# Context tokens of a diffusion layer: one pair of k tiles turned at once, the other seven in a lane beside the products

## The chip, the cores and the metric

The kernel runs on one core of a Trainium2 chip. A time is the device time of one execution in microseconds (us). The engines of the core are TensorE (PE; its weight loads are shown as PEld), VectorE (DVE), ScalarE (ACT), GpSimd (POOL) and SyncE (SP), which issues nearly all transfers. They run side by side and wait for each other by semaphores.

## The reference

One layer of a diffusion model for 256 latent tokens `x` and 256 context tokens `ctx`, width D = 2048, in float32. The part that the change touches is the first one: all 512 tokens are normalised by their root mean square, scaled and shifted by terms that are computed from a condition vector, and multiplied by one wide weight matrix.

```python
def rms_norm(x, g):
    y = xf * lax.rsqrt(jnp.mean(xf * xf, axis=-1, keepdims=True) + NORM_EPS)
    return y * g
def modulate(h, shift, scale):
    return h * (1 + scale) + shift
def ada_terms(cond, w_ada, b_ada):
    return jnp.split(jax.nn.silu(cond) @ w_ada + b_ada, 6, axis=-1)
# c conditions the latent tokens, c_ctx the context tokens
# z = modulate(rms_norm(tokens, norm1_g), shift, scale);  proj = z @ w_in
# columns of w_in: keys and values (latent and context tokens) | queries | gates (latent only)
```

Behind it come two kinds of attention of the latent tokens over all 512 tokens, a gated merge, a second normalisation and a gated MLP with a convolution of width 3. Their code is the same in both kernels.

## The kernel before

**Tiling.** A k tile is 128 of the 2048 rows of `w_in`; there are 16. Tokens come in with the tokens on the partitions, so each 128 x 128 piece has to be turned by PE (a matmul with the identity `ident`, L227) before it can be an operand whose contraction runs over D. The turned and normalised tokens `xn` lie in the slots X0 to X3, four k tiles each, latent and context side by side. A pair of k tiles of the context takes four transposes into one PSUM bank (two k tiles by two halves of the tokens) and then one scaling on DVE by `rb`, the reciprocal root mean square spread over the partitions.

**Products.** Each float32 operand is split in two parts, `hi` (a rounded copy, made by ACT) and `lo` (the rest, a DVE subtraction), and each product is the sum of three matmuls, hi x hi, hi x lo, lo x hi (`mm` at L218). The weights pass through a ring of four raw buffers (`raw`) and three buffers each of `hi` and `lo`. In the trace `sZL` is the modulated operand of the latent tokens, `sZC` that of the context tokens; `make_z` makes both parts of each: for each k tile ACT makes hi, DVE multiplies in place, DVE subtracts.

**Chunks and blocks.** The k tiles are taken in five chunks of 2, 3, 3, 4 and 4 tiles. In each chunk the blocks of columns follow each other: `a` and `b` (keys and values, both kinds of token), `c` and `d` (queries) and the gate blocks `0` to `3`. Chunk 0 has the order `cd012ab3`, the next two `abcd0123`, chunk 3 `abcd`, chunk 4 begins with `b` and `d`. Block results are added up in SBUF by DVE (evacuations such as `sK<-bank,sK`).

**Modulation values.** For each chunk a GEMV (`gemv_chunk`) takes the columns of `w_ada` for the chunk's k tiles through the same ring of raw buffers and multiplies them with the condition vectors `cs` (L409 in the rows, four steps for a chunk of three or four tiles), after which ACT copies the sums to `scratch`, PE turns them (`bank<-ident,scratch`) and three DVE operations make `md`, the shift and scale of that chunk. `make_z` of a chunk can't begin before its `md`.

**What sets the order.** PE's instructions stand in the order in which the program emits them. A small planner (`Pace`) interleaves side jobs, called lanes, with the products: it keeps a model of the work that DVE and ACT still have, lets it shrink by the modelled time of each product, and takes a step of a lane where the modelled rest of DVE and of ACT is at most the lane's limit and where a distance that the lane asked for by its last `yield` has passed on PE. Lanes of smaller `prio` go first. `finish` runs a lane to its end at once. Lanes of the first chunks are `lane_ctx` (the context's preparation), `lane_mods` (GEMV steps, with a distance of 4, 10, 14 and 14 us between the steps of chunks 1 to 4) and `lane_z` (the operands of the next chunk). The order on DVE and ACT follows from a scheduler that goes by the emitted order and the dependencies.

In chunk 0 the context's tokens are loaded ahead of gate block 0 and `lane_ctx` is added; the lane is finished ahead of block `a`, the first that needs it. In chunk 0, `lane_mods` and `lane_z` are added at the same place. A chunk ends with

```python
        while ci + 1 not in mods:
            next(gm)
        finish(nxt)
```

so that GEMV steps which found no place between the blocks, and what is left of the next operands, are emitted there in one go.

Of the kernel before, what the change touches and what calls it, by code (L numbers as in the profile page):

```python
# [9 lines left out]
F32 = mybir.dt.float32  # L10
# [6 lines left out]
P = 128  # L17
D = 2048
KT = D // P
T = 256  # L20
# [9 lines left out]
CHUNKS = (2, 3, 3, 4, 4)  # L30
# [3 lines left out]

ORDER0, ORDERM, CTX_AT = "cd012ab3", "abcd0123", 2

CTX_LIM, NXT_LIM, GM_LIM, LIM_EVAC, LIM_ATT, LIM_LAT = 0.1, 0.8, 2.0, 2.0, 3.0, 1.3
REST_LIM, REST_LIM_B, REST_LIM_Q, REST_LIM_A, REST_LIM_W, REST_LIM_U = 0.65, 0.6, 1.7, 0.5, 1.4, 0.5
REST_CI, REST_AFTER, REST_DMA = 1, 6.0, 6.0
GAPS = (0.0, 4.0, 10.0, 14.0, 14.0)  # L40
# [10 lines left out]
class Pace:  # L51
# [50 lines left out]
    def run(self, gen):  # L102
        for _ in gen:
            self.tick()

    def finish(self, *gens):

        gens = list(gens)
        self.lanes = [x for x in self.lanes if not any(x[0] is g for g in gens)]
        while gens:  # L110
            gens = [g for g in gens if next(g, None) is not None]
# [39 lines left out]
def _build(tc, nc, es, a):  # L151
    pace = Pace()
    PE, POOL = nc.tensor, nc.gpsimd
    ACT, DVE = Engine(nc.scalar, pace, "act"), Engine(nc.vector, pace, "dve")
    run, finish = pace.run, pace.finish
# [5 lines left out]
    tmp = es.enter_context(tc.tile_pool(name="tmp", bufs=3))  # L161
    psum = es.enter_context(tc.tile_pool(name="psum", bufs=8, space=bass.MemoryType.PSUM))

    def bank():
        return psum.tile([P, 512], F32, tag="bank", name="bank")

    def slot(tag, shape, dt=F32):
        return big.tile(shape, dt, tag=tag, name=f"s{tag}")

    def small(n, tag="st", bufs=8):  # L170
        return tmp.tile([P, n], F32, tag=tag, name=tag, bufs=bufs)

    def scratch(shape, dt=F32):
        return tmp.tile(shape, dt, tag="P", name="scratch", bufs=4)
# [40 lines left out]
    def mm(out, lhsT, rhs, start, stop):  # L215
        n = free(rhs)
        pace.tensor(n * 0.417e-3 if rhs.dtype == F32R else max(n, 256) * 1.67e-3)
        PE.matmul(out, lhsT, rhs, start=start, stop=stop, skip_group_check=True)  # L218
# [6 lines left out]
    def transpose(out, src, n=P):  # L225
        pace.tensor(0.11)
        PE.transpose(out, src, ident[:n, :n])  # L227
# [16 lines left out]
    def rstd(out, sums, n, cnt, extra=None):  # L244
        m = small(8)
        DVE.tensor_scalar(out=m[:, :n], in0=sums, scalar1=1.0 / cnt, scalar2=EPS, op0=ALU.mult, op1=ALU.add)
        POOL.tensor_tensor(out=out, in0=m[:, :n], in1=mhalf[:, :n], op=ALU.pow)
        if extra is not None:
            DVE.tensor_scalar(out=out, in0=out, scalar1=extra, scalar2=None, op0=ALU.mult)


    xin = [slot(g, [P, D]) for g in ("ZC0", "K2", "G2", "G3")]

    def load_tokens(cnd):
        src = a["ctx"][0] if cnd else a["x"][0]
# [10 lines left out]
    def silu_c():  # L266
        ex = tmp.tile([P, 2, 16], F32, tag="cex", bufs=1, name="cex")
        ACT.activation(ex, craw, AF.Exp, scale=-1.0)
        DVE.tensor_scalar(out=ex, in0=ex, scalar1=1.0, scalar2=None, op0=ALU.add)
        DVE.reciprocal(ex, ex)  # L270
        DVE.tensor_mul(cs.rearrange("p j c -> p c j")[:, 0:2, :], craw, ex)
# [55 lines left out]
    xn = [slot(f"X{i}", [P, 4, NTOK]) for i in range(4)]  # L327

    def norm_tokens(cnd, fills=None):
        rb = scratch([P, T])  # L330
        rr = []

        def spread(t, ss):
            r = small(1)
            rstd(r, ss, 1, D)
            rt = tmp.tile([P, P], F32, tag="rr", name="rr", bufs=2)
            DVE.tensor_copy(rt, r.broadcast_to([P, P]))
            rr.append(rt)

        for t in range(2):  # L340
            ss = small(1)
            if cnd == 0:
                junk = slot(f"G{t}", [P, D])
                ACT.activation(junk, xin[t], AF.Square, accum_out=ss)
            else:
                s4 = small(4)
                for i in range(4):
                    ACT.activation(scratch([P, 512]), xin[2 + t][:, i * 512:(i + 1) * 512], AF.Square,
                                   accum_out=s4[:, i:i + 1])
                    yield 0.0  # L350
                DVE.reduce_sum(ss, s4, axis=AX.X)
            spread(t, ss)

        def turn(k2):
            ps = bank()
            for k in range(2):
                for t in range(2):
                    transpose(ps[:, (2 * k + t) * P:(2 * k + t + 1) * P],
                              xin[2 * cnd + t][:, (k2 + k) * P:(k2 + k + 1) * P])
            return k2, ps  # L360

        def scale(k2, ps):
            DVE.tensor_mul(xn[k2 // 4][:, k2 % 4:k2 % 4 + 2, cnd * T:(cnd + 1) * T],
                           ps.rearrange("p (k t) -> p k t", t=T), rb[:, None, :].broadcast_to([P, 2, T]))

        ahead = 2 if cnd == 0 else 1
        pend = [turn(k2) for k2 in range(0, 2 * ahead, 2)]
        yield 4.0
        if cnd == 0:
            silu_c()  # L370
        rbp = bank()
        for t in range(2):
            mm(rbp[:, t * P:(t + 1) * P], rr[t], ident, t == 0, True)
        ACT.copy(rb, rbp[:, 0:T])
        yield 1.0
        if cnd == 0:

            fills.extend((turn, scale, k2) for k2 in range(2 * ahead, KT, 2))
        for k2 in () if cnd == 0 else range(2 * ahead, KT, 2):
            scale(*pend.pop(0))  # L380
            pend.append(turn(k2))
            yield 0.5
        for p in pend:
            scale(*p)
            yield 0.0

    w_ada = a["w_ada"][0].rearrange("(p j) c -> p j c", j=16)
    starts = [sum(CHUNKS[:i]) for i in range(len(CHUNKS))]
# [44 lines left out]
    def make_z(ci, cnd):  # L433
        kt0, nk = starts[ci], CHUNKS[ci]
        md = mods[ci]
        zt = slot(("ZL", "ZC")[cnd] + str(ci % 2), [P, 2, nk, T], F32R)
        zs[ci][cnd] = zt
        c = slice(cnd * T, (cnd + 1) * T)
        for k in range(nk):
            kt = kt0 + k  # L440
            x = xn[kt // 4][:, kt % 4, c]
            s1, s2 = md[:, 1, k, cnd:cnd + 1], md[:, 0, k, cnd:cnd + 1]
            ACT.activation(zt[:, 0, k, :], x, AF.Identity, bias=s2, scale=s1)
            DVE.tensor_scalar(out=x, in0=x, scalar1=s1, scalar2=s2, op0=ALU.mult, op1=ALU.add)
            DVE.tensor_sub(zt[:, 1, k, :], x, zt[:, 0, k, :].bitcast(F32))
            if late:
                l, src, h = late.pop()
                DVE.tensor_sub(l, src, h.bitcast(F32))
            yield 0.0
# [87 lines left out]
    def group_T(ps, w, mov, first, last):  # L537
        wh, wl = w
        mh, ml = mov
        for n in range(wh.shape[1] // P):  # L540
            mm3(ps[n // 2][:, (n % 2) * T:(n % 2 + 1) * T], wh[:, n * P:(n + 1) * P], wl[:, n * P:(n + 1) * P],
                mh, ml, first and n % 2 == 0, last)
# [97 lines left out]
    def block_g(cis, g):  # L640
        if cis[0] == 0:
            gates[g] = slot(f"G{g}", [P, 8, T])
        ps = [bank() for _ in range(4)]
        ks = [(ci, k) for ci in cis for k in range(CHUNKS[ci])]
        for i, (ci, k) in enumerate(ks):
            group_T(ps, take(), zk(zs[ci][0], k), i == 0, i == len(ks) - 1)
            yield
        evac(f"g{g}", cis[0] == 0, [(gview(g, n), ps[n]) for n in range(4)])
# [77 lines left out]
    def lane_z(ci):  # L726
        while ci not in mods:
            yield 0.3
        for cnd in range(2):
            yield from make_z(ci, cnd)  # L730

    with tc.manual_schedule(engines={ENG.DVE, ENG.Activation}):
        fills, turned = [], []
# [24 lines left out]
        for scale, p in turned:  # L758
            scale(*p)

    def lane_ctx():
        yield from norm_tokens(1)
        yield from make_z(0, 1)

    gm = lane_mods()
    for ci in range(nch - 1):
        nxt = lane_z(ci + 1)
        lc = None
        if ci > 0:
            pace.add(nxt, limit=NXT_LIM)  # L770
        if ci == REST_CI:
            pace.add(rest, after=REST_AFTER, limit=REST_LIM, dma=REST_DMA, prio=9)
        if ci == 2:
            pace.add(lane_tables(), after=5.0, limit=1.0, prio=8)
        for i, b in enumerate(order(ci)):
            if ci == 0 and i == CTX_AT:
                load_tokens(1)
                lc = pace.add(lane_ctx(), after=CTX_AFTER, limit=CTX_LIM, prio=0)
                pace.add(gm, limit=GM_LIM, prio=2)
                pace.add(nxt, limit=NXT_LIM)  # L780
            if lc is not None and b in "ab":
                finish(lc)
                lc = None
            run(block_g([ci], int(b)) if b in "0123" else {"a": block_a, "b": block_b, "c": block_c, "d": block_d}[b](ci))
        while ci + 1 not in mods:
            next(gm)
        finish(nxt)
    last = nch - 1
    zo, zl_ = f"ZL{nch % 2}", f"ZL{last % 2}"
# [735 lines left out]
```

## Time and profile before

| | |
|---|---|
| time, median of 3 runs | 1538.22 us (1536.16 to 1539.11) |
| the profiled execution | 1534.41 us, of it the span of the trace 1532.6 us |
| PE busy | 1501.6 us, 98% of the span |
| PEld, DVE, ACT, POOL busy | 86%, 72%, 50%, 1% |
| DMA, main queue | 348.96 MB, 65.4% of 16 engines' span |

How to read it: busy is the time in which an engine had an instruction, whatever the others did. PE and PEld overlap. Times in a timeline count from the start of the span; ends of matmuls are modelled, so two neighbours on PE can overlap on paper, and the distance from one start to the next is the better measure of what one costs.

### The profile page before, as it was taken

To read this page: it belongs to the slowest core of one execution; us is meant where nothing else is said; L and a number is where in the kernel's file an instruction comes from. 1 tells how busy PE (TensorE), PEld (TensorE's weight loads), DVE (VectorE), ACT (ScalarE), POOL (GpSimd) and SP (SyncE) were. 2 spreads that over 40 slices of the span, in tenths; PEclk is the share of its full clock that TensorE was granted. 3 is DMA by queue.
4 is the path that set the end of the run, shared out by engine and by line. 5 is a ranking of instruction groups with operands and counts; after the bars stand their busy time and mean duration, and the time that the engine had idled before them with its cause. 6 is when DMAs were issued, how large, how long until landed. Compare 5 with 4: busy or idle time off the path is not lost.

```text
span 1532.6 us, 23197 instructions
## 1 busy us (share of the span) xinstructions
PE 1501.6 (98%) x9361; PEld 1316.5 (86%) x9361; DVE 1099.8 (72%) x1554; ACT 764.3 (50%) x1144; POOL 15.2 (1%) x23
## 2 busy tenths in 40 slices
PE   7999999999999999999989999999999999999997
PEld 5788888899999999998889888888888888888885
DVE  4457786798778887788878989667656666555556
ACT  4534242455775446643456545555545555444444
POOL 0000000010000000000000000000000000000000
PEclk9999999999999999999999999999999999999999
DMA  9779788655347784498957878655565565555552
GB/s 361 248 271 337 280 311 300 244 183 193 111 158 241 270 291 154 148 319 295 347 209 247 302 266 291 212 193 183 174 198 188 175 209 189 194 194 192 192 196 79
DMA packets 123708, 350.44 MB, mean 229 GB/s; under 512 B 6750, under 2 KB 20296, under 8 KB 117072
## 3 DMA queue, kind: packets, MB, share of 16 engines
q1 hardware_dynamic: 123600, 348.96, 65.4%
q8 instruction: 73, 1.20, 0.3%
q14 instruction: 35, 0.29, 0.1%
HBM read 346.84 MB, written 2.10 MB: 228 GB/s over the span
## 4 chain that ended last, share of the span: by engine, by line
PE 91%; DMA 4%; DVE 3%; ACT 1%; issue 1%; SPq 0%; ACTq 0%; POOLq 0%; POOL 0%; DVEq 0%
PE bank L218 88%; DMA raw<-in_w_ada 2%; PE bank L227 2%; PE bank L409 2%; DVE sK L140 1%; DVE acc L140 1%; ACT scratch L140 0%; DVE lo L140 0%; DMA sK<-in_x 0%; DMA raw<-in_w_in 0%; DMA raw<-in_w_out 0%; DVE sX L140 0%; DVE scratch L140 0%; ACT hi L140 0%; SPq L403 0%
## 5 line engine op out<-in xcount | busy, mean ns | idle before, releaser
L140 ACT CAST hi<-raw 128x1024 fp32r<-128x1024 f32 (+2 forms) x462 | 470.9, 1022 | 580.0 <-PE bank L218 511.9
L140 DVE TENSOR_TENSOR lo<-raw,hi 128x1024 fp32r<-128x1024 f32 (+2 forms) x463 | 548.0, 1187 | 294.0 <-ACT hi L140 292.8
L218 PE MATMUL bank<-sZL,hi 128*128 128x256 f32 (+2 forms) x2528 | 536.8, 313 | 1.3 <-ACT sZL L140 0.9
L218 PEld LDWEIGHTS bank<-sZL,hi 128*128 128x128 f32 (+1 forms) x2528 | 408.3, 191 | 28.8 <-issue 8.4
L218 PE MATMUL bank<-sZL,lo 128*128 128x256 f32 (+1 forms) x1648 | 386.9, 283 | 0.5 <-DVE lo L140 0.4
L218 PEld LDWEIGHTS bank<-sZL,lo 128*128 128x128 f32 (+1 forms) x1648 | 290.7, 190 | 14.6 <-DVE lo L140 0.9
L218 PE MATMUL bank<-hi,sZC 128*128 128x512 f32 (+1 forms) x816 | 261.2, 383 | 0.0
L218 PE MATMUL bank<-sX,hi 128*128 128x512 f32 (+1 forms) x896 | 235.1, 364 | 0.0
L218 PEld LDWEIGHTS bank<-hi,sZC 128*128 128x128 f32 x816 | 152.5, 188 | 30.0
L218 PEld LDWEIGHTS bank<-sX,hi 128*128 128x128 f32 x896 | 154.0, 190 | 15.6 <-issue 1.0
L140 DVE SCALAR_TENSOR_TENSOR acc<-raw,cs,acc 128x1024 f32<-128x1024 f32 x120 | 153.5, 1279 | 15.6 <-DMA raw<-in_w_ada 14.9
L218 PE MATMUL bank<-lo,sZC 128*128 128x512 f32 (+1 forms) x344 | 131.3, 382 | 0.0
L218 PEld LDWEIGHTS bank<-sX,lo 128*128 128x128 f32 x704 | 110.5, 189 | 13.6
L218 PE MATMUL bank<-sX,lo 128*128 128x256 f32 x704 | 119.9, 281 | 0.0
L218 PEld LDWEIGHTS bank<-lo,sZC 128*128 128x128 f32 x344 | 64.7, 188 | 12.4 <-DVE lo L140 0.2
L140 DVE TENSOR_TENSOR sK<-bank,sK 128x512 f32<-128x512 f32 (+1 forms) x92 | 60.0, 683 | 8.8 <-PE bank L218 6.4
L218 PE MATMUL bank<-hi,sZL 128*128 128x512 f32 x192 | 63.3, 392 | 0.0
L218 PE MATMUL bank<-sZC,hi 128*128 128x256 f32 x256 | 50.2, 283 | 1.4 <-DVE sZC L140 1.4
L218 PE MATMUL bank<-hi,sX 128*128 128x512 f32 x128 | 50.6, 396 | 0.0
L218 PE MATMUL bank<-lo,sX 128*128 128x512 f32 x128 | 50.1, 392 | 0.1
L140 DVE TENSOR_TENSOR sG<-bank,sG 128x512 f32<-128x512 f32 x64 | 41.6, 681 | 3.9 <-PE bank L218 3.9
L218 PEld LDWEIGHTS bank<-hi,sZL 128*128 128x128 f32 x192 | 36.1, 188 | 9.4 <-ACT hi L140 1.2
(203 smaller groups left out, 1397.6 us busy)
## 6 DMA issues: line engine op xcount, KB each, us to landing
raw<-in_w_up SPq DMA_DIRECT2D x88, 1024.0 KB, 5.0
raw<-in_w_ada SPq DMA_DIRECT2D x80, 1024.0 KB, 7.1
raw<-in_w_down SPq DMA_DIRECT2D x44, 1024.0 KB, 5.4
raw<-in_w_in SPq DMA_DIRECT2D x37, 1024.0 KB, 5.4
raw<-in_w_out SPq DMA_DIRECT2D x16, 1024.0 KB, 7.1
raw<-in_w_ada SPq DMA_DIRECT2D x16, 768.0 KB, 5.7
raw<-in_w_br_b SPq DMA_DIRECT2D x8, 1024.0 KB, 5.9
raw<-in_w_br_a SPq DMA_DIRECT2D x8, 1024.0 KB, 5.6
```

Source lines behind the costliest of these rows:

```text
L140: return f(*args, **kw)
L218: PE.matmul(out, lhsT, rhs, start=start, stop=stop, skip_group_check=True)
L227: PE.transpose(out, src, ident[:n, :n])
L409: PE.matmul(ps[32 * g:32 * g + 32, :cols], cs[:, j0 + jj, :], w[:, jj, :], start=j0 + j == 0, stop=j0 + j == 14, skip_group_check=True)
```

## The change

The limit of the context's lane goes from 0.1 to 1.0. The raw context's first half lies in the slot Y0 and no longer in G2 (which gate block 2 evacuates into), and `rb` gets a tile of its own, as it now lives longer. `norm_tokens(1)` turns and scales one pair of k tiles only, those of chunk 0; the other seven pairs go to a list. A new lane takes the pairs of that list one by one (turn, a distance of 1.0, scale, a distance of 0.5). It is added where `lane_ctx` has been finished, and run to its end behind the last block of chunk 0. `lane_z` waits, before it makes the context's operands of a chunk, until the k tiles of that chunk are turned.

```diff
-CTX_LIM, NXT_LIM, GM_LIM, ... = 0.1, 0.8, 2.0, ...
+CTX_LIM, NXT_LIM, GM_LIM, ... = 1.0, 0.8, 2.0, ...
-    xin = [slot(g, [P, D]) for g in ("ZC0", "K2", "G2", "G3")]
+    xin = [slot(g, [P, D]) for g in ("ZC0", "K2", "Y0", "G3")]
     def norm_tokens(cnd, fills=None):
-        rb = scratch([P, T])
+        rb = tmp.tile([P, T], F32, tag="rb", bufs=1, name="rb")
...
-        ahead = 2 if cnd == 0 else 1
-        pend = [turn(k2) for k2 in range(0, 2 * ahead, 2)]
+        pend = [turn(k2) for k2 in ((0, 2) if cnd == 0 else (0,))]
...
-        if cnd == 0:
-            fills.extend((turn, scale, k2) for k2 in range(2 * ahead, KT, 2))
-        for k2 in () if cnd == 0 else range(2 * ahead, KT, 2):
-            scale(*pend.pop(0))
-            pend.append(turn(k2))
-            yield 0.5
+        fills.extend((turn, scale, k2) for k2 in range(2 * len(pend), KT, 2))
         for p in pend:
             scale(*p)
             yield 0.0
     def lane_z(ci):
...
         for cnd in range(2):
+            while cnd and ctx_turned[0] < starts[ci] + CHUNKS[ci]:
+                yield 0.3
             yield from make_z(ci, cnd)
+    ctx_turned, more_ctx = [2], []
     def lane_ctx():
-        yield from norm_tokens(1)
+        yield from norm_tokens(1, more_ctx)
         yield from make_z(0, 1)
+    def lane_ctx_more():
+        while more_ctx:
+            turn, scale, k2 = more_ctx.pop(0)
+            p = turn(k2)
+            yield 1.0
+            scale(*p)
+            ctx_turned[0] = k2 + 2
+            yield 0.5
...
             if lc is not None and b in "ab":
                 finish(lc)
                 lc = None
+                more = pace.add(lane_ctx_more(), limit=1.0, prio=1)
...
         while ci + 1 not in mods:
             next(gm)
+        if ci == 0:
+            finish(more)
         finish(nxt)
```

The first place at which the order moves is the end of gate block 2 of chunk 0, where the preparation of the context is finished. Before, PE turns seven pairs of k tiles there (28 transposes) between the `rr` products that spread the reciprocal root mean square and the first product with `sZC`; now it does no transposes of its own there beside the four of the first pair, and four more stand behind block `a`, four behind block `b` and twenty at the end of the chunk. The GEMV's second step for chunk 1 (the eight products with `raw,cs`, 32x384) moves from behind gate block 1 to behind gate block 2.

The second place is the end of chunk 0 on PE: gate block 3, the last block, and what stands behind it. `sZL_248` is the latent operand of chunk 0, `sZL_848` or `sZL_890` and `sZC_925` are those of chunk 1, and `sY`, `sG` the two halves of the raw context. Before:

```order
L218 MATMUL bank<-sZL_248,hi 128x256 x2
L218 MATMUL bank<-sZL_248,lo 128x256
L218 MATMUL bank<-sZL_848,hi 128x256 x2
L218 MATMUL bank<-sZL_848,lo 128x256
L218 MATMUL bank<-sZC_925,hi 128x256 x2
```

Now:

```order
L218 MATMUL bank<-sZL_248,hi 128x256 x2
L218 MATMUL bank<-sZL_248,lo 128x256
L227 MATMUL bank<-ident,sY_90 128x128
L227 MATMUL bank<-ident,sG_91 128x128
L227 MATMUL bank<-ident,sY_90 128x128
L227 MATMUL bank<-ident,sG_91 128x128
L227 MATMUL bank<-ident,scratch 128x128 x3
L403 MATMUL bank<-raw,cs 32x384 x8
L227 MATMUL bank<-ident,sY_90 128x128
L227 MATMUL bank<-ident,sG_91 128x128
```

Behind these rows the last two go on in turn until sixteen transposes of the context have followed the GEMV's products, and then come `sZL_890` and `sZC_925`. The transposes of the modulation values (`ident,scratch`) and a GEMV step of the next chunk, which before stood ahead of gate block 3, now stand behind it.

The same place on DVE, where `lo` is the low part of a weight, `sX` the normalised tokens and `rb` the spread reciprocal. Before:

```order
L140 TENSOR_TENSOR md_831<-bank_827,vec_98 128x2x6
L140 TENSOR_TENSOR md_831<-bank_827,md_831 128x2x6
L140 SCALAR_TENSOR_TENSOR md_831<-md_831,vec_98 128x6
L140 TENSOR_TENSOR lo_863<-raw_860,hi_862 128x576
L140 TENSOR_SCALAR sX0_104<-sX0_104,md_831 128x256 x2
L140 TENSOR_TENSOR sZL1_848<-sX0_104,sZL1_848 128x256 x2
L140 TENSOR_SCALAR sX1_105<-sX1_105,md_831 128x256
L140 TENSOR_SCALAR sX0_104<-sX0_104,md_831 128x256
L140 TENSOR_TENSOR sZL1_848<-sX1_105,sZL1_848 128x256
L140 TENSOR_TENSOR sZC1_925<-sX0_104,sZC1_925 128x256
```

Now:

```order
L140 TENSOR_TENSOR sX1_105<-bank_862,rb_424 128x2x256
L140 TENSOR_TENSOR md_873<-bank_869,vec_98 128x2x6
L140 TENSOR_TENSOR lo_943<-raw_940,hi_942 128x576
L140 TENSOR_TENSOR md_873<-bank_869,md_873 128x2x6
L140 SCALAR_TENSOR_TENSOR md_873<-md_873,vec_98 128x6
L140 TENSOR_TENSOR sX2_106<-bank_898,rb_424 128x2x256
L140 TENSOR_SCALAR sX0_104<-sX0_104,md_873 128x256 x2
L140 TENSOR_TENSOR sZL1_890<-sX0_104,sZL1_890 128x256 x2
L140 TENSOR_TENSOR sX2_106<-bank_904,rb_424 128x2x256
L140 TENSOR_TENSOR sX3_107<-bank_910,rb_424 128x2x256
L140 TENSOR_TENSOR sX3_107<-bank_916,rb_424 128x2x256
L140 TENSOR_SCALAR sX1_105<-sX1_105,md_873 128x256
```

Five scalings of the context (`bank,rb`) now stand among the operations that make the operands of chunk 1, and `sZC1_925` comes three rows behind the last row shown, after `sX0` and `sZL1`.

The third place is the end of chunk 3 on PE, block `d`, whose latent operand is `sZL_2191` before and `sZL_2324` now. Before:

```order
L218 MATMUL bank<-lo,sZL_2191 128x512
L218 MATMUL bank<-hi,sZL_2191 128x512
L227 MATMUL bank<-ident,scratch 128x128 x4
L218 MATMUL bank<-hi,sZL_2191 128x512
L218 MATMUL bank<-lo,sZL_2191 128x512
```

Now, with `sZL_3011` the first operand of chunk 4:

```order
L218 MATMUL bank<-lo,sZL_2324 128x512
L218 MATMUL bank<-hi,sZL_2324 128x512
L227 MATMUL bank<-ident,scratch 128x128 x4
L218 MATMUL bank<-hi,sZL_3011 128x512
L218 MATMUL bank<-lo,sZL_3011 128x512
```

Before, 24 products of block `d` follow the transposes of the modulation values; now none does.

DVE at the end of chunk 3, with `sK` the evacuations of blocks and `acc` the accumulation of another GEMV. Before:

```order
L140 TENSOR_TENSOR lo_2944<-raw_2922,hi_2943 128x1024
L140 TENSOR_TENSOR md_2966<-bank_2961,vec_98 128x16
L140 TENSOR_TENSOR md_2966<-bank_2961,md_2966 128x16
L140 SCALAR_TENSOR_TENSOR md_2966<-md_2966,vec_98 128x8
L140 TENSOR_TENSOR lo_2980<-raw_2977,hi_2979 128x1024
L140 TENSOR_SCALAR sX3_107<-sX3_107,md_2966 128x256 x2
```

Now:

```order
L140 TENSOR_TENSOR sK3_313<-bank_2922,sK3_313 128x512
L140 TENSOR_TENSOR md_3007<-bank_3002,vec_98 128x16
L140 TENSOR_TENSOR sK3_313<-bank_2923,sK3_313 128x512
L140 TENSOR_TENSOR md_3007<-bank_3002,md_3007 128x16
L140 TENSOR_TENSOR lo_3044<-raw_3041,hi_3043 128x1024
L140 SCALAR_TENSOR_TENSOR md_3007<-md_3007,vec_98 128x8
L140 TENSOR_TENSOR sK3_313<-bank_2924,sK3_313 128x512
L140 SCALAR_TENSOR_TENSOR acc_2681<-raw_2981,cs_86,acc_2681 128x1024
L140 TENSOR_SCALAR sX3_107<-sX3_107,md_3007 128x256 x2
```

Evacuations of block `d`, a weight's low part and an accumulation now stand between the three operations of `md` and ahead of the first multiply of `make_z`. On SP, the loads of `lane_tables` come later in the program, in the second chunk's stretch.

## Rows read from the trace of the kernel before

**Rows 1.** The page: busy time, share of the span, instructions.

```profile
PE 1501.6 (98%) x9361; PEld 1316.5 (86%) x9361; DVE 1099.8 (72%) x1554; ACT 764.3 (50%) x1144; POOL 15.2 (1%) x23
```

**Rows 2.** PE's waits, 27 to 300: waiting, releaser; us in total, times, longest.

```profile
PE bank L218 <- DVE sZC L140: 1.4, 1, 1.4
PE bank L409 <- DMA raw<-in_w_ada: 1.1, 2, 0.9
```

**Rows 3.** Timeline 57 to 67: start, us, operation, count [idle before, releaser].

```profile
57.58 1.50 PE L409 MATMUL bank<-raw,cs 128*32 128x384 f32 x16
...
59.50 0.61 PE L218 MATMUL bank<-ident,rr 128*128 128x128 f32 x4
59.94 4.40 PE L227 MATMUL bank<-ident,sG 128*128 128x128 f32 x28
60.15 0.37 ACT L140 COPY scratch<-bank 128x256 f32<-128x256 f32 x1 [1.19 <-PE bank L218]
60.55 4.87 DVE L140 TENSOR_TENSOR sX<-bank,scratch 128x512 f32<-128x512 f32 x8 [0.33 <-ACT scratch L140]
61.28 1.09 ACT L140 ACTIVATE sZC<-sX,md 128x256 fp32r<-128x256 f32 x2 [0.76 <-DVE sX L140]
65.34 0.73 DVE L140 TENSOR_SCALAR sX<-sX,md 128x256 f32<-128x256 f32 x2
65.98 0.75 DVE L140 TENSOR_TENSOR sZC<-sX,sZC 128x256 fp32r<-128x256 f32 x2
66.45 0.39 PE L218 MATMUL bank<-sZC,hi 128*128 128x256 f32 x1 [1.43 <-DVE sZC L140]
66.68 0.28 PE L218 MATMUL bank<-sZC,lo 128*128 128x256 f32 x1
...
67.03 0.28 PE L218 MATMUL bank<-sZL,lo 128*128 128x256 f32 x1
```

**Rows 4.** Timeline of PE where chunk 1 first reads its context operand.

```profile
88.35 0.40 PE L218 MATMUL bank<-sZC,hi 128*128 128x256 f32 x2
```

**Rows 5.** Timeline at the end of chunk 3.

```profile
291.89 0.60 PE L227 MATMUL bank<-ident,scratch 128*128 128x128 f32 x4
...
292.53 0.18 DVE L140 TENSOR_TENSOR md<-bank,vec 128x16 f32<-128x16 f32 x1 [0.85 <-PE bank L227]
...
293.15 2.08 ACT L140 ACTIVATE sZL<-sX,md 128x256 fp32r<-128x256 f32 x4
...
299.18 0.39 PE L218 MATMUL bank<-hi,sZC 128*128 128x512 f32 x1
299.41 0.39 PE L218 MATMUL bank<-lo,sZC 128*128 128x512 f32 x1
```

**Rows 6.** Costs by line, 27 to 320: busy, mean ns; idle before, releasers.

```profile
L140 DVE TENSOR_TENSOR lo<-raw,hi 128x1024 fp32r<-128x1024 f32 x55 | 66.8, 1221 | 29.5 <-ACT hi L140 29.0
L140 DVE TENSOR_TENSOR sK<-bank,sK 128x512 f32<-128x512 f32 x51 | 33.4, 684 | 6.5 <-PE bank L218 6.4
L140 DVE SCALAR_TENSOR_TENSOR acc<-raw,cs,acc 128x1024 f32<-128x1024 f32 x25 | 31.9, 1278 | 4.9 <-DMA raw<-in_w_ada 4.8
L140 DVE TENSOR_TENSOR lo<-raw,hi 128x576 fp32r<-128x576 f32 x12 | 9.1, 755 | 15.3 <-ACT hi L140 15.3
```

**Rows 7.** The page's transfers: KB each, us from issue to landing.

```profile
raw<-in_w_ada SPq DMA_DIRECT2D x16, 768.0 KB, 5.7
```

**Rows 8.** Timeline of PE further on, around 776.

```profile
776.20 0.61 PE L227 MATMUL bank<-ident,scratch 128*128 128x128 f32 x2 [2.17 <-DVE scratch L140]
...
778.10 1.54 PE L227 MATMUL bank<-ident,scratch 128*128 128x128 f32 x6 [1.28 <-DVE scratch L140]
...
781.07 0.63 PE L218 MATMUL bank<-sZL,hi 128*128 128x256 f32 x2
...
781.71 0.63 PE L218 MATMUL bank<-sZL,hi 128*128 128x256 f32 x2
```

**Rows 9.** One stretch: us; PE, PEld, DVE, ACT, POOL busy; clock; DMA share, GB/s.

```profile
782.00:784.00 2.00, 2.00 (x14) 2.00 (x14) 2.00 (x3) 0.57 (x1) 0.00 (x0) 0.71 0.00 0
```

More of the change, by code (lines that the diff above doesn't have):

```diff
@@ L35 @@
 ORDER0, ORDERM, CTX_AT = "cd012ab3", "abcd0123", 2
-CTX_LIM, NXT_LIM, GM_LIM, LIM_EVAC, LIM_ATT, LIM_LAT = 0.1, 0.8, 2.0, 2.0, 3.0, 1.3
+CTX_LIM, NXT_LIM, GM_LIM, LIM_EVAC, LIM_ATT, LIM_LAT = 1.0, 0.8, 2.0, 2.0, 3.0, 1.3
 REST_LIM, REST_LIM_B, REST_LIM_Q, REST_LIM_A, REST_LIM_W, REST_LIM_U = 0.65, 0.6, 1.7, 0.5, 1.4, 0.5
```

## The prediction

> **What bounds the kernel now.** First the page: TensorE (PE) is busy for 98% of the span [rows 1] and runs in the order in which the program is written, so the end moves by what PE waits more or less, and hardly by anything else. Then PE's waits between 27 us (first products) and 300 us (last context operand made): the reader is to see that they are few and short, 1.4 us for the context's operand sZC and 1.1 us for two loads of w_ada [rows 2]. So all that this change can win by taking waits away is some 2.5 us. Third the timeline of the context's preparation [rows 3]: 28 transposes in 4.40 us, 0.157 us each without a gap, then 1.43 us of wait for sZC. Last the ends of chunk 0 and of chunk 3, where the operands of the next chunk are made. In both the reader is to see that PE goes on without a wait, because the modulation values `md` are ready well before: at the end of chunk 0 PE first reads the new sZC at 88.35 with no idle time in front [rows 4]; at the end of chunk 3 the `md` transposes start at 291.89, while 24 products of block d are still to come, and sZC is first read at 299.18 [rows 5].
>
> **The change, part by part.** In the changed order I call T1 the end of gate block 2 in chunk 0, T0 the end of gate block 3 (the last of chunk 0) and T3 the end of block d in chunk 3 (the last there).
>
> *The transposes.* Still 32 of them, on PE. 4 stand at T1, 4 each behind blocks a and b, 20 at T0. A transpose between products takes PE's time as well, so 28 x 0.157 leaves one place and comes back in others: 0. Bounds: 0.1 us for each of the four places worse, or 4.4 us better if the products covered them (a rival below).
>
> *The lane starts sooner and the GEMV step after it* (limit 1.0 for 0.1). The second GEMV step of chunk 1 moves from behind gate block 1 to T1, one block later; its load then has 6 us more, and the longest wait for w_ada, 0.9 us, goes [rows 2]: -0.95. Bounds -1.1 (both waits) and 0.
>
> *The wait for sZC at T1.* The chain is still bare: from the two rr products (59.50) to the ACT copy (60.15), the scaling (60.55; eight take 4.87, so 0.61 each), ACT's sZC (61.28, about 0.57 each), then DVE's multiply (0.40) and subtraction (0.42) [rows 3]. With one scaling instead of eight: copy at R+0.65, scaling to R+1.7, ACT to R+2.35, multiply to R+2.75, subtraction to R+3.2. PE has only 0.3 (rr) + 0.36 + 0.12 (four products of 0.12, the pitch of 256 columns: three from 66.68 to 67.03) to do meanwhile, since the 28 transposes that covered the chain are gone: it waits 2.45 instead of 1.43, +1.0. Bounds 0 and 1.5.
>
> *The end of chunk 0.* With GEMV a block later, `md` for chunk 1 comes only at T0, and 20 transposes of context stand there too. PE: 4 transposes to T0+0.6, 3 for `md` to 1.1, a GEMV step (1.5 [rows 3]) to 2.6, four times 4 transposes to 3.3, 3.9, 4.5 and, as the last bank is freed by a scaling at 4.1, 5.1. DVE in its order: scaling 0.8 to 1.45, first `md`, a weight's lo of 576 columns (0.755 [rows 6]) to 2.4, `md` done at 2.8, scaling (it needs PE's 3.3) to 4.1, sZL of two k to 5.5 (a pair of multiplies 0.73 and a pair of subtractions 0.75 with 0.08 of overlap), three more scalings to 7.4, four operations of 0.33 to 0.42 to 8.85, of which the last is sZC of the first k. PE has a free bank and sZL at 6.2, does four products to 6.7, and waits for sZC until 8.9. Of 8.9 us PE works 5.6: +3.3. Bounds: 1.5 (if only the last wait counts) and 5. Its own load is no more: a w_ada load of 768 KB lands 5.7 us after issue [rows 7], and it can be issued when the step before ends, a block of 5.8 us (48 x 0.12) and the transposes ahead.
>
> *The end of chunk 3.* The GEMV of chunk 4 also ends later, and `md` moves from the middle of block d to T3, with nothing of chunk 3 left. Transposes to T3+0.6. DVE meanwhile has a lo (1.22) and two evacuations (0.684 each, less when back to back [rows 6]) to 1.05, as the weight's cast before the lo waits for a buffer that PE frees at T3-2.7. Then `md` 0.2, evacuation 0.65, `md` 0.2, lo 1.2, `md` 0.2: 3.5. ACT makes the first sZL by 4.1, all four by 5.6 (2.08 for four [rows 5]), then four of sZC. DVE goes on with an evacuation, an accumulation (1.278 [rows 6]) to 5.4, multiplies to 6.1, first subtraction 6.5, the second pair of k to 8.25, multiplies for sZC to 8.9, first sZC 9.3. PE: waits 0.6 to 4.1, 2 products, waits to 6.55 for sZL's low part, 6 products (0.23 each, from 299.18 and 299.41 [rows 5]) to 7.9, waits to 9.35, 4 products to 10.25. Of 10.25 it works 0.6 + 12 x 0.23: +6.9. Before, nothing was lost there. Bounds: 4 (if the lo and the accumulation fell behind the z operations) and 8.2 (if the cast's buffer or load is 1.3 later).
>
> *The clock after it.* The trace shows what such waits do further on: before 776 PE waited 2.17, transposed, waited 1.28 [rows 8], and from then products of 256 columns came at 0.21 us (three from 781.07 to 781.71) instead of 0.12; the stretch 782 to 784 is still at a granted 0.71, so part of it at 1.2 GHz and part at 2.4 [rows 9]. Some 15 products until 783 took 0.21 for 0.12: 1.4, with the transposes (six in 1.54 for 0.157 each) 1.75. At T3 the waits are longer (3.5, 2.0, 1.45), so I take 1.75 there, and none at T0 (1.1 and 2.2, shorter than those). Bounds 0 and 3.5 (both places). The Trainium skill, "TensorE: Matmul & The Clock Gate", section "HAM oscillation — how this bites in real kernels", says that a TensorE that runs out of work between bursts (there, waiting for DMA) drops to half rate and begins each burst cold. If the rule held for every wait, T0 and T1 would pay as well; with 1.75 at each the sum would be 15.5 instead of 12.0. The trace agrees at 776, but not at 66.45, where after 1.43 of wait the products still came at 0.12 [rows 3].
>
> *Edits at nothing.* rb has a tile of its own and the raw context lies in Y0 instead of G2: the two loads are issued at the same place, and gate block 2's evacuation need no longer wait for the transposes, which held no product back. SP issues the table loads in chunk 1 instead of chunk 0; they stand behind a clearing of X0 that waits for the last z operation at T0+10, and behind them the weights of block c, which PE needs after blocks a and b, 90 x 0.12 + 36 x 0.23 = 19 us later than T0+8.9; without that cover a load's 5 to 6 us would show. The later lanes fall in other places by some us; I give them 0, with +-1.5.
>
> The sum: -0.95 + 1.0 + 3.3 + 6.9 + 1.75 = +12.0. Against its own profiled time, 1534.41 (span 1532.6 and 1.8 around it), 1546.4. That execution was 3.8 faster than the median shown, 1538.22, so a median run should be at **1550**.
>
> **Rivals.** (1) *Only one end is bare.* If DVE and ACT at T3 are ahead of PE, so that `md` and z meet little queue, T3 costs 2 or so and the clock stays: +5, 1543. For it: before, DVE did the same work within 7 us without holding PE. Against: then 24 products lay beside it. (2) *The weights come late.* The stream of loads is moved from chunk 0 to 4 and some GEMV step or cast waits for its load, as in chunk 0 before, at several steps; T0 loses the clock too: +17, 1555. For it: a load takes 5.7 us [rows 7]. Against: two such waits in all before. (3) *The other side: the products cover the transposes.* If transposes beside products cost PE nothing and DVE's scalings are done beside them, the 4.40, the 1.43 and the 0.95 all go: -6.8, 1531. It decides if the four at T1 leave PE free and `md` is not later than T0-6. Against: PE does one after the other at 0.157, and the order puts `md` behind the block. (4) *No change:* the 3.3 is given back because the loads, now ahead, no longer hold PE in chunks 1 and 2, and T3 costs under 2: 1539.
>
> **Chances.** The forecast 0.66, (1) 0.13, (2) 0.12, (3) 0.04, (4) 0.05. The range of the likeliest is 1546 to 1553; to hold 8 in 10 it reaches 1544 (T3 4, T0 1.5 and no clock: +6) to 1556 (T0 5, T3 8.2 and clock twice, +17, nearly). Slower by over 0.2% (3.1 us, about what can be told from no change here) is the forecast, (1), (2) and a part of (4): 0.92. Within it 0.05, faster 0.03.
>
> **What would show it.** Right: no wait for w_ada in chunk 0; a wait of 2 to 2.5 for sZC at T1; two waits for sZL and sZC behind the transposes after gate block 3; after block d of chunk 3, four transposes and then waits of 3.5, 2 and 1.5 us with a granted clock under 1 behind them. Wrong: PE going from block d of chunk 3 into block b of chunk 4 without a wait, or transposes that take no time between blocks.

## The result and the profile after

| | before | changed |
|---|---|---|
| median, four runs each | 1538.19 us (1536.16 to 1539.11) | 1553.29 us (1550.21 to 1556.67) |
| ratio, 95% interval | | 1.0093 (1.0077 to 1.0109) |
| profiled execution, its span | 1534.41, 1532.6 | 1555.22, 1553.4 |

The change costs 15.1 us by the medians, 14.3 by the ratio; the forecast was 1550 in a range of 1544 to 1556. In a second set of runs (e8 below) the ratio was 1.0101 (1.0086 to 1.0117), 15.5 us. The profiled execution of before lies 3.8 us under its median, that of the changed kernel 1.9 over, so the two spans are 20.8 apart: a difference between two traces can hold some 5 us of scatter, and where times and traces differ below, the times decide.

The changed kernel's busy times on the page (us, share of the span, instructions):

```profile
PE 1509.2 (97%) x9361; PEld 1323.8 (85%) x9361; DVE 1099.6 (71%) x1554; ACT 764.4 (49%) x1144; POOL 14.6 (1%) x23
```

The work is the same to the instruction as in [rows 1]. PE is 7.6 us busier, as the granted clock was low for longer (below), and idle for 13 us more. Its waits from 27 to 330 (us in total, times, longest), which answer [rows 2]:

```profile
PE bank L218 <- ACT sZL L140: 5.2, 1, 5.2
PE bank L403 <- DMA raw<-in_w_ada: 2.3, 2, 1.2
PE bank L218 <- DVE sZC L140: 2.2, 2, 1.7
PE bank L218 <- ACT sZC L140: 1.5, 1, 1.5
PE bank L218 <- DVE sX L140: 1.3, 1, 1.3
PE bank L218 <- DVE sZL L140: 0.9, 1, 0.9
...
```

Timeline of the changed kernel where the context is prepared, against [rows 3] (T1 of the forecast):

```profile
54.07 0.27 PE L227 MATMUL bank<-ident,sY 128*128 128x128 f32 x1
54.18 0.27 PE L227 MATMUL bank<-ident,sG 128*128 128x128 f32 x1
...
56.03 0.71 PE L218 MATMUL bank<-ident,rr 128*128 128x128 f32 x4
56.77 0.37 ACT L140 COPY rb<-bank 128x256 f32<-128x256 f32 x1 [1.09 <-PE bank L218]
57.18 0.69 DVE L140 TENSOR_TENSOR sX<-bank,rb 128x512 f32<-128x512 f32 x1 [0.73 <-ACT rb L140]
...
58.56 0.39 PE L218 MATMUL bank<-sZC,hi 128*128 128x256 f32 x1 [1.47 <-ACT sZC L140]
59.47 0.38 PE L218 MATMUL bank<-sZC,hi 128*128 128x256 f32 x1 [0.52 <-DVE sZC L140]
```

A transpose now follows the one before after 0.11 us, not 0.157, and the bare chain costs 1.99 us of wait (1.47 and 0.52) against 1.43. The end of chunk 0, against [rows 4], first the timeline, then PE's granted clock in stretches of 2 us (columns as in [rows 9]):

```profile
82.01 0.49 PE L227 MATMUL bank<-ident,scratch 128*128 128x128 f32 x3
...
86.47 1.88 DVE L140 TENSOR_TENSOR sX<-bank,rb 128x512 f32<-128x512 f32 x3
...
87.30 0.48 PE L218 MATMUL bank<-sZL,hi 128*128 128x256 f32 x2 [1.35 <-DVE sX L140]
...
89.24 0.42 DVE L140 TENSOR_TENSOR sZC<-sX,sZC 128x256 fp32r<-128x256 f32 x1
...
89.72 0.58 PE L218 MATMUL bank<-sZC,hi 128*128 128x256 f32 x1 [1.71 <-DVE sZC L140]
...
95.39 0.40 PE L218 MATMUL bank<-sZL,hi 128*128 128x256 f32 x2
```

```profile
86.00:88.00 2.00, 0.70 (x4) 0.54 (x4) 2.00 (x5) 2.00 (x6) 0.00 (x0) 1.00 1.00 409
88.00:90.00 2.00, 0.29 (x2) 0.28 (x2) 2.00 (x7) 0.92 (x2) 0.00 (x0) 0.62 1.05 396
90.00:92.00 2.00, 2.00 (x10) 2.00 (x11) 1.97 (x5) 0.00 (x0) 0.52 (x1) 0.50 1.05 372
```

The two waits are 3.06 us, and behind them the clock is at 0.50, the 1.2 GHz level: the 26 products from 89.72 to 95.39 took 5.67 us, 2.55 more than the 26 x 0.12 = 3.1 that they take at the pitch of [rows 3]. The end of chunk 3, against [rows 5], in the same two views:

```profile
301.35 0.60 PE L227 MATMUL bank<-ident,scratch 128*128 128x128 f32 x4
302.25 0.17 DVE L140 TENSOR_TENSOR md<-bank,vec 128x16 f32<-128x16 f32 x1
...
304.07 1.04 ACT L140 CAST hi<-raw 128x1024 fp32r<-128x1024 f32 x1 [4.19 <-DMA raw<-in_w_in]
305.14 1.23 DVE L140 TENSOR_TENSOR lo<-raw,hi 128x1024 fp32r<-128x1024 f32 x1 [2.04 <-ACT hi L140]
306.29 0.16 DVE L140 SCALAR_TENSOR_TENSOR md<-md,vec 128x8 f32<-128x8 f32 x1
306.48 2.08 ACT L140 ACTIVATE sZL<-sX,md 128x256 fp32r<-128x256 f32 x4 [1.37 <-DVE md L140]
307.14 0.80 PE L218 MATMUL bank<-hi,sZL 128*128 128x512 f32 x1 [5.19 <-ACT sZL L140]
...
309.28 1.22 PE L218 MATMUL bank<-hi,sZL 128*128 128x512 f32 x2 [0.92 <-DVE sZL L140]
```

```profile
302.00:304.00 2.00, 0.00 (x0) 0.00 (x0) 1.10 (x4) 0.00 (x0) 0.00 (x0) 1.00 1.05 348
...
308.00:310.00 2.00, 1.08 (x3) 0.63 (x3) 2.00 (x7) 2.00 (x6) 0.00 (x0) 0.50 0.30 37
310.00:312.00 2.00, 2.00 (x6) 1.29 (x5) 2.00 (x7) 0.53 (x2) 0.00 (x0) 0.50 0.95 385
```

The last operation of `md` stands behind the low part of a weight, whose cast waited until 304.07 for its load: 5.19 us without a product, then the chain of `make_z` with no product beside it, at half clock. In the second trace of the same kernel (e8) that load was in time, and PE waited 3.04 and 0.92 there. The clock fell before the first product (0.85 from 304 to 306 in e8), so that the first products came every 0.43 us instead of 0.23: from the `md` transposes to the end of the twelve products of the forecast PE took 9.99 us in e8, where the kernel before takes 3.08 for the same work.

Lastly, the two rows of PE (before, then changed) between which lies the second half of the kernel, from block a of chunk 4 to a product far in the MLP:

```profile
328.57 0.40 PE L218 MATMUL bank<-sZC,hi 128*128 128x256 f32 x2
...
1282.76 0.40 PE L218 MATMUL bank<-hi,sZC 128*128 128x512 f32 x1
```

```profile
342.50 0.40 PE L218 MATMUL bank<-sZC,hi 128*128 128x256 f32 x2
...
1303.58 0.40 PE L218 MATMUL bank<-hi,sZC 128*128 128x512 f32 x1
```

This stretch takes 954.19 us before and 961.08 after, 6.89 more, though no line of the edit is about it. Three places of the changed kernel's timeline in it which before has not, or shorter (2.17 for the last, [rows 8]):

```profile
429.24 1.58 PE L218 MATMUL bank<-sK,sX 128*128 128x256 f32 x11 [0.65 <-DVE sK L140]
...
431.88 0.38 PE L218 MATMUL bank<-ident,rr 128*128 128x128 f32 x1 [0.62 <-DVE rr L140]
...
796.01 0.69 PE L227 MATMUL bank<-ident,scratch 128*128 128x128 f32 x2 [2.92 <-DVE scratch L140]
```

How far the changed trace is behind at the first context product of each chunk: +1.25 us at chunk 1 (89.72 against 88.35 + 0.12, as it is the second product), +4.20 at chunk 2 (172.72, 168.52), +2.73 at chunk 3 (250.13, 247.40), +11.97 at chunk 4 (311.15, 299.18), +13.93 at 342.50, +20.82 at 1303.58.

### The profile page after: what moved, and what is told of

Its sections match the earlier page's. It is cut to its first block, busy times and chain, and to the rows that moved or that the text cites. A ratio compares the mean times of both kernels' runs of the same rounds, so it can differ in the third digit from the quotient of the medians.

```text
span 1553.4 us, 23199 instructions
## 1 busy us (share of the span) xinstructions
PE 1509.2 (97%) x9361; PEld 1323.8 (85%) x9361; DVE 1099.6 (71%) x1554; ACT 764.4 (49%) x1144; POOL 14.6 (1%) x23
## 4 chain that ended last, share of the span: by engine, by line
PE 88%; DVE 5%; DMA 4%; ACT 1%; issue 1%; POOL 0%; SPq 0%; ACTq 0%; POOLq 0%; DVEq 0%
PE bank L218 84%; DMA raw<-in_w_ada 2%; PE bank L227 2%; PE bank L403 2%; DVE lo L140 2%; DMA raw<-in_w_in 1%; DVE sK L140 1%; DVE acc L140 1%; DMA raw<-in_w_out 1%; DMA sK<-in_x 0%; DVE sX L140 0%; ACT hi L140 0%; DVE sG L140 0%; DVE scratch L140 0%; ACT scratch L140 0%
```

## The experiments

Times are ratios to the kernel before on the same chip, with the 95% interval; 0.001 is 1.5 us. "Second half" is the stretch just defined, from one trace, less the 954.19 us of before.

**e1: slots alone.** The kernel before with

```diff
-    xin = [slot(g, [P, D]) for g in ("ZC0", "K2", "G2", "G3")]
+    xin = [slot(g, [P, D]) for g in ("ZC0", "K2", "Y0", "G3")]
-        rb = scratch([P, T])
+        rb = tmp.tile([P, T], F32, tag="rb", bufs=1, name="rb")
```

> The kernel before with the raw context's first half in Y0 and rb in a tile of its own, and nothing else. My theory: neither holds PE, so 0 (within 1.5 us of the kernel before; its trace also shows how far two traces of the same order differ). Rival (the slot matters: gate block 2 or the table loads now wait for something): 2 us or more slower, with a new wait of PE in chunk 0 or 1.

Measured 0.9988 (0.9973 to 1.0003): no difference. But its trace shows why a transpose had cost 0.157 us. In the kernel before, ACT copies the four banks of gate block 2 into G2 only behind the transposes that read the raw context there; in e1 it does so ahead of them (before, then e1):

```profile
64.27 2.05 ACT L140 COPY sG<-bank 128x512 f32<-128x512 f32 x4 [1.90 <-PE bank L227]
```

```profile
55.52 2.74 ACT L140 COPY sG<-bank 128x512 f32<-128x512 f32 x4 [0.17 <-PE bank L218]
```

So in the kernel before four banks fewer were free for the transposes, and from the third group of four on each waited for a scaling to give a bank back. The weight loads of before's own trace show that wait, which the merged row of [rows 3] hides:

```profile
61.89 0.42 PEld L227 LDWEIGHTS bank<-ident,sG 128*128 128x128 f32 x4 [0.18 <-DVE sX L140]
```

In e1 the same 28 transposes come every 0.11 us, and PE then waits longer for sZC:

```profile
67.23 0.38 PE L218 MATMUL bank<-sZC,hi 128*128 128x256 f32 x1 [3.41 <-DVE sZC L140]
```

So the 4.40 us of [rows 3] were partly wait: 28 x 0.047 = 1.3. The end of that place is set by eight scalings on DVE (4.87 us in both traces).

**e2: the limit alone.** e1 with

```diff
-CTX_LIM = 0.1
+CTX_LIM = 1.0
```

> e1 with the context lane's limit at 1.0; all eight pairs are still turned in that lane. My theory (the late end of chunk 3 comes from the limit, which puts a GEMV step one block later, and costs 11 us there): slower than before by 10 to 15 us, with PE's wait of some 5 us for sZL before the first product of chunk 4 and the granted clock under 1 behind it; at the end of chunk 0 the bare chain of md and z without the scalings, 1 to 3 us. Rival (the cost comes from the pairs that are turned later, by the split): within 2 us of before and no such wait.

Measured 1.0135 (1.0112 to 1.0158), 20.8 us and not 10 to 15, more than the whole change: PE waits 3.35 and 0.72 us for sZL ahead of chunk 4, 2.5 us in three waits at the end of chunk 0, and its second half is 12.2 us longer. The limit costs, and the change as a whole, which has the split too, costs a quarter to a third less. By the traces most of that lies in the second half (12.2 against 6.9 and 6.0), for which e6 has the reason.

**e3: the split alone.** The changed kernel with

```diff
-CTX_LIM = 1.0
+CTX_LIM = 0.1
```

> The changed kernel with the limit back at 0.1: the split, the lane and the slots stay. My theory: the md of every later chunk stands where it stood before, so the end of chunk 3 costs nothing; the end of chunk 0 has twenty transposes and five scalings but its md early, so it costs 0 to 3 us, and the transposes cost 1.3 us less than before, as they no longer go at DVE's pace: between 2 us faster and 3 us slower than before. Rival (the split is what costs): 8 us or more slower.

Measured 0.9981 (0.9968 to 0.9994): 2.9 us faster than before. No wait of PE is left at the end of chunk 0 and none at chunk 4; `md` of chunk 1 is ready ahead of gate block 3, and PE has no wait over 0.3 us among the twenty transposes there.

**e4: the late `md` of chunk 4 undone.** The changed kernel with

```diff
-GAPS = (0.0, 4.0, 10.0, 14.0, 14.0)
+GAPS = (0.0, 4.0, 10.0, 14.0, 12.0)
```

> The changed kernel with the distance between the GEMV steps of chunk 4 at 12 us for 14, so that the md transposes of chunk 4 stand in block d, where they were before. My theory: the wait for sZL of 5.2 us, the 0.9 us behind it and the low clock there go, 10 to 12 us less than the changed kernel, so 3 to 6 us above before. Rival (the stream of loads is late, and PE would wait for it wherever md stands): the wait moves to another operand or load, and less than 4 us are gained.

Measured 0.9998 (0.9985 to 1.0010), level with before and some 15 us under the changed kernel: more than I expected. The `md` transposes stand in block d (297.91 in its trace), PE has no wait from 280 to 330, and the waits at 429 and 431 us are gone too. Counted back from the end, PE's matmuls stand as in the kernel before for 7432 of the 9361 in the trace, that is from 278 us, in chunk 3, on; in the changed kernel only the last 4064 do, from 768 us on (both times as in before's trace). One number moved two things.

**e5: the late `md` of chunk 4 alone.** The kernel before with

```diff
-GAPS = (0.0, 4.0, 10.0, 14.0, 14.0)
+GAPS = (0.0, 4.0, 10.0, 14.0, 16.0)
```

> The kernel before (context turned in one go, old limit, old slots) with one number changed: the distance between the GEMV steps of chunk 4 is 16 us for 14, which puts the md transposes of chunk 4 behind block d of chunk 3, as in the changed kernel. My theory (the place of this md alone makes the loss at the end of chunk 3 and what follows from it, some 13 us): 9 to 15 us slower than before, with a wait of 3 to 5 us for sZL before chunk 4, the clock at half behind it, and new small waits around 430 us and 775 us. Rival (the load stream that the split moves is needed for it): within 3 us of before.

Measured 1.0042 (1.0028 to 1.0056), 6.5 us and not 9 to 15. The waits are there:

```profile
304.20 0.79 PE L218 MATMUL bank<-hi,sZL 128*128 128x512 f32 x1 [3.35 <-ACT sZL L140]
305.74 1.22 PE L218 MATMUL bank<-hi,sZL 128*128 128x512 f32 x2 [0.32 <-DVE sZL L140]
```

and the mean clock from 300 to 310 is 0.68. But its second half is only 1.6 us longer, with before's order in it. My theory that the late `md` brings the later losses fell here.

**e6: the pairs ahead of gate block 3.** e4 with

```diff
+            if ci == 0 and b == "3":
+                finish(more)
             run(block_g([ci], int(b)) if b in "0123" else ...)
...
-        if ci == 0:
-            finish(more)
```

> e4 (limit 1.0, distance 12) with the context's pairs finished ahead of gate block 3 instead of behind it, so that no scaling stands in the chain of md and z at the end of chunk 0; md stays there. My theory (of the 3.1 us of waits there the scalings make the smaller part, since md is late whatever they do): PE still waits for the first sZL and sZC of chunk 1, 1.5 to 2.5 us instead of 3.1, and with waits that short the clock may hold: 0.5 to 3 us less than e4. Rival (the scalings are the whole cost of that place): no wait is left there, 4 to 6 us less than e4.

Measured 1.0085 (1.0069 to 1.0101): 13 us slower where both theories said faster. The waits at the end of chunk 0 are 0.65, 0.53 and 1.35 instead of 1.35 and 1.71, so the scalings had been the smaller part of them, as thought; chunk 4 starts without a wait. The loss is in the second half, 10.5 us, with the longest wait of PE in that trace, and on DVE the reason: the product behind the output projection waits for the gate that the `rest` lane makes (the program finishes the lane there, behind the projection's last matmul). PE first, then DVE:

```profile
784.61 1.88 PE L218 MATMUL bank<-acc,ones 128*128 128x512 f32 x4
...
792.39 0.69 PE L227 MATMUL bank<-ident,scratch 128*128 128x128 f32 x2 [5.90 <-DVE scratch L140]
```

```profile
786.29 0.69 DVE L140 TENSOR_TENSOR scratch<-bank,sK 128x512 f32<-128x512 f32 x1 [6.65 <-ACT sK L140]
```

The products with `acc,ones`, which make the gate, stand behind the projection's last product there; in the kernel before they stand 7 us ahead of it (at 766.67, the last product at 773.65).

`rest` (the accumulations `acc`, which make the modulation of the second half and the gate in that `sK`) is placed by the planner in what room is left. Where DVE's order comes to the `rr` of the compressed keys' norm, some 415 to 435 us into the span (the expectations of e9 and e10 call that place the second normalisation), it has made 28 of its 128 accumulations in before, e3, e4 and e5, 29 in the changed kernel, 27 in e2 and e6; kernels with the same count have the same PE order through the whole second half. That made the new theory for e9 to e11.

**e7: a GEMV step over the wait for sZC.** e3 with

```diff
+            if ci == 0 and b == "2":
+                lane = [x for x in pace.lanes if x[0] is gm][0]
+                lane[1] = 1e9
             if lc is not None and b in "ab":
                 finish(lc)
+                next(gm)
+                lane[1] = pace.pe + GAPS[1]
```

> e3 (split, limit 0.1) with the second GEMV step of chunk 1 placed by hand behind the rr products, where PE waits for sZC; one block later than in e3. My theory: the step's 1.5 us lie over the 2.0 us of wait for sZC, and its load is there in time, so the 1.2 us of wait for w_ada go too: 1 to 3 us less than e3. Rival (the wait goes elsewhere, to the next GEMV load or to the ACT copy): within 0.5 us of e3.

Measured 0.9986 (0.9974 to 0.9998), no different from e3, though the interval does not exclude a gain of 1 us. The trace is as the rival has it: PE still waits 0.46 and 1.35 us for sZC behind the step, and the 1.19 us of wait for w_ada ahead of the step before it stay.

**e8: the changed kernel again.**

> The changed kernel as it is, on the same chip as e5 to e7, for its distance to them and a second trace. My theory: 13 to 17 us slower than before, with the same waits at the ends of chunk 0 and chunk 3 and around 430, 775 and 796 us, as they follow from the order. Rival (what the first trace has beyond 14 us is scatter of one execution): the waits at 430 to 796 us are gone in this trace.

Measured 1.0101 (1.0086 to 1.0117), with the same waits at the end of chunk 0, at 428 and 431 and at 793 (2.93); at chunk 4 they are shorter by the load that was late in the first trace. Second half: 6.0 us longer than before. Those waits are no scatter. The two short ones near 775 (0.56 and 0.76 in the first trace, for parts of a weight) are not there, and others stand at 704 and 748 (1.29 and 0.45): those do change from one execution to the next.

**e9: the changed kernel with the `rest` lane in step.**

```diff
-REST_CI, REST_AFTER, REST_DMA = 1, 6.0, 6.0
+REST_CI, REST_AFTER, REST_DMA = 1, 6.0, 5.5
```

> The changed kernel with one number of another lane changed: the accumulation lane (acc) may take a step only while the planner's rest of transfers is under 5.5 us instead of 6. It then has made 28 accumulations instead of 29 at the second normalisation, and from chunk 4 on every PE instruction stands as in the kernel before; the ends of chunk 0 and chunk 3 stay as the change has them. Theory after e5 and e6 (about half of the loss is not at the two ends but comes from that lane being out of step in the second half): 5 to 8 us less than the changed kernel, 6 to 9 us above before, without the waits around 430 us and with 2.2 us instead of 2.9 before the last transposes of the second normalisation. Rival (all of the loss is at the ends): within 2 us of the changed kernel.

Measured 1.0059 (1.0038 to 1.0080): 9.1 us above before, 5 to 6.5 under the changed kernel. The waits around 430 are gone, that at 789 is 2.17, the second half 3.2 us longer than before instead of 6.9; the waits at both ends are as in the changed kernel (1.35 and 1.71; 3.35 and 0.81).

**e10: the kernel before with that lane out of step.** The same line with 7.0.

> The kernel before with the same number at 7 for 6: the accumulation lane has made 29 accumulations there, and from chunk 4 on every PE instruction stands as in the changed kernel; the md of chunk 4 stays in block d, and the context is turned as before. Theory (the lane's step alone costs): 5 to 8 us slower than before, with waits of 0.6 us for sK and rr around 410 to 420 us. Rival: within 2 us of before.

Measured 1.0043 (1.0029 to 1.0058), 6.6 us. It is less clean than meant: in its trace 5.2 us are lost by block a of chunk 4 (0.66 us more wait at the transposes of chunk 0 and a clock of 0.50 from 68 to 70, GEMV loads waited for in chunk 2), and 4.4 in the second half, with 0.65 for sK, 0.64 for rr and 2.92 at 784. So the order with 29 accumulations costs by itself.

**e11: e6 with the lane in step.** The same line with 8.0.

> e6 with the same number at 8, which brings its lane from 27 to 28 accumulations, so that from the end of chunk 3 on PE's order is that of the kernel before. Theory: the 11 us that e6 lost to before go nearly whole (8 to 12 us less than e6), and what is left is the end of chunk 0: within 3 us of before. Rival (finishing the pairs ahead of gate block 3 costs by itself): 5 us or more above before.

Measured 1.0032 (1.0019 to 1.0044), 8 us less than e6, but 4.9 above before and not within 3. The second half lost 3.9 instead of 10.5. What remains lies in chunks 0 and 1: waits of 1.16, 0.53 and 1.34 at the end of chunk 0, and in chunk 1 loads of w_ada of 0.76, 0.88 and 3.13.

The second half by the lane's count, over all traces: with 28 accumulations 0.8 to 4.0 us longer than in the trace of before (e1, e3, e4, e5, e7, e9, e11), with 29 4.4 to 6.9 (e10, e8, the changed kernel), with 27 10.5 and 12.2 (e6, e2). The means, with before's 0 among the first, are 1.8, 5.8 and 11.3: one accumulation more costs some 4 us, one fewer some 9.5.

Of the 4 us two can be read as waits (0.65 and 0.62 near 430, and 2.92 for 2.17 behind the output projection). Another part goes with the clock: behind that last wait it stays at 0.50 longer in all three traces with 29. The changed kernel, then the kernel before, both 8 to 10 us behind the wait's end:

```profile
804.00:806.00 2.00, 2.00 (x14) 2.00 (x13) 0.54 (x2) 0.56 (x1) 0.00 (x0) 0.68 0.95 274
```

```profile
784.00:786.00 2.00, 2.00 (x19) 2.00 (x18) 1.01 (x3) 1.36 (x2) 0.00 (x0) 1.00 0.87 229
```

Of the traces with 28 only e11 has the clock as low for as long there.

## Why the prediction was right, and where it was not

The sign and the size were right, and two of the three places where time is lost, the ends of chunk 0 and of chunk 3, were named with their cause; the third, the second half, was not. So the sum, 12.0, came out near for reasons that were only partly those given.

*The transposes, at 0:* they cost 1.3 us less than taken. Their 0.157 us "without a gap" was a misreading: the banks came free late, as e1 shows.

*w_ada at T1, -0.95:* right, that wait is gone. *The wait for sZC there, +1.0:* +0.56 (1.99 against 1.43).

*The end of chunk 0, +3.3:* the waits are 3.06 us. Of the two causes in the forecast, the late `md` is shown: e3 has `md` early and no wait, and e2, e6 and e11 have it late without the scalings in the chain and keep 2.5 to 3.0 us. The scalings, which the working needed to reach 3.3, add 0.6 at most. What also failed is "none at T0" for the clock: it fell in every trace with these waits (the changed kernel twice, e4 and e9, and e2, e6 and e11 with three waits) and cost 2.55 us in the first. The Trainium skill ("TensorE: Matmul & The Clock Gate", "HAM oscillation — how this bites in real kernels") has TensorE begin at half rate after waits between bursts, there for DMA; the rows at T0 agree with it, for waits on VectorE.

*The end of chunk 3, +6.9, and the clock, +1.75:* right in cause and size, not in its parts. Of the three waits forecast (3.5, 2.0 and 1.45) the second trace has two, 3.04 and 0.92; the rest of the time went into slow products, as the clock had fallen ahead of the first. (The 1.75 is not what its own numbers give either: 1.4, and six transposes in 1.54 instead of 0.94, are 2.0.) From the start of chunk 3 to block a of chunk 4 the changed kernel loses 11.2 us in its first trace (2.2 of it the late load) and 8.4 in the second, against 8.65 in the sum. By the times the late `md` costs 6.5 us alone (e5) and 9.4 by the distance of e9 from e4, two kernels whose PE order differs at that place and no more behind it.

*The later lanes, "I give them 0, with +-1.5":* this is the step that failed most. The second half costs some 4 us by its order alone: with one accumulation more before the norm of the compressed keys, PE has another order there. Nothing in the sum stood for it. What made up for part of it: the terms of chunk 0 add up to +3.35 in the sum (-0.95, 1.0 and 3.3), and e4, which has all of them, is level with before by its times (-0.3). To that extent the near hit is luck.

*The rivals.* (1), only one end bare, and (4), no change, fell with the waits at both ends. (2), loads late, was real but small: waits for w_ada of 2.3 us in chunk 1, of which chunk 2 gives 1.5 back. (3), the products cover the transposes, did not come true in the changed kernel, whose transposes took 0.11 us each of PE's time.

The measured time can be added up from kernels that differ in one step each: from before to e4 -0.3 us; from e4 to e9, the late `md`, 9.4; from e9 to the changed kernel, the lane out of step, 5.2 to 6.5. Together that is the 14.3 to 15.5 measured. Each of these steps has an interval of 2 to 4 us. In the -0.3 two things cancel: the split, which gains 2.9 (e3), and the limit with the late `md` of chunk 1, which costs 2.6 (e4 against e3, not clear of noise). Why 27 and 29 accumulations are worse than 28 is shown for one wait only (e6, the gate that is late for the output projection); for the waits near 430 it stays open.

The change is two changes. The split with the old limit (e3) is 2.9 us faster than the kernel before; the limit undoes that and costs the rest.

## What to carry to other kernels

In a kernel whose order comes from a planner, a local edit has to be followed to the end of the order, not to the end of the stage: compare the two orders row by row and ask of every place where they differ, however far on, what work is bare there. A value that is made for the next stage should have products behind it; when a lane slips by one step, the first thing to look for is the deadline at which what is left of it is done with nothing beside it.

## What was unexpected of the hardware

The same waits do not always cost the clock. The 1.47 and 0.52 us at T1 left it at 1.00 in the changed kernel's first trace; in the second, with the same two waits, it was 0.50 from 60 to 62 and 0.73 from 62 to 64. Of the seven traces with these two waits (1.46 or 1.47, then 0.52 or 0.53) the clock fell in three: e3, e4 and e8. In e1 a wait of 3.41 us left it at 1.00. And of one kernel's executions, same program and chip, the fastest and the slowest lie 9 us apart (e1: 1535.24 to 1544.10): with its 12 executions against 29 of before the interval is still 2.3 us to either side.
